# Weight products ordered by part: the high tile's products first, a third high tile, one late weight pool, and held-back gathered rows

## The chip, the core and the metric

The kernel runs on one core of a Trainium2 chip. The metric is the device time of one execution in microseconds (us); less is better. The core has a matrix engine (PE), a vector engine (DVE), a scalar engine (ACT), a general engine (POOL) and an engine that only issues transfers (SP). Each engine takes its instructions in the order in which the program lists them; they wait for each other through semaphores. Transfers are issued from queues (here of SP, ACT and POOL) and share 16 DMA engines. Tiles live in an on-chip memory; matrix results land in eight accumulator banks.

## What is computed

One layer of a hybrid block on 512 tokens of width 2048, in f32, in three parts with a residual and a layer norm after each:

```python
h = hybrid_mixer(x, ...)            # x @ w_in (12 pieces), an mLSTM of 4 heads, forgetting attention of 16 heads,
                                    # two gated branches, and @ w_out
x = layer_norm(DN_ALPHA * x + h, ln_w[l, 0], ln_b[l, 0])
h = memory_cross_attention(x, mem, w_xq, w_xkv, w_xo)   # 4 heads over 256 memory rows
x = layer_norm(DN_ALPHA * x + h, ln_w[l, 1], ln_b[l, 1])
h = peer_ffn(x, w_pq, sub_keys, expert_u, expert_v)     # 16384 experts; each token and head takes its best 16
x = layer_norm(DN_ALPHA * x + h, ln_w[l, 2], ln_b[l, 2])
```

In `peer_ffn` a query picks expert rows by two top-16 searches; the result is `sum_k gelu(u_k . x) * g_k * v_k` over the 128 picked experts of a token.

## The kernel before

**Products in three parts.** PE multiplies a rounded f32 type. To keep f32 accuracy every operand is split into a high part (rounded) and a low part (the rest), and each product is done as high·high + high·low + low·high, three matmuls into one bank (`mm3`, lines 150 to 153). Activations are split once; weights are split as they stream through.

**The weight stream.** All weights come as tiles of 128x1024 f32, 512 KB each. `load_w` (line 136) does this for each tile: SP issues the load into a `raw` tile (line 130); ACT writes the high part `whi` (line 123); DVE (line 126), or POOL (line 125) for every fourth tile while `work["share"]` is 4, subtracts to give the low part `wlo`. Each of `raw`, `whi` and `wlo` is a ring of a few tiles. A slot of `raw` is free for the next load when the subtraction has read it; a slot of `whi` or `wlo` is free when the last matmul that reads it has ended. The ring sizes are set by `weights(stack, raw, hi, lo)`: 5, 2, 2 for the first part (`W_FIRST`), 6, 2, 3 for the second (`W_NEXT`), 3, 2, 2 for the third (line 961) and 5, 2, 2 for the rest (line 996).

**Products of one tile.** `group_as` (line 169) holds an activation block still and streams 512 weight columns: for one block of 128 tokens a tile gives 6 matmuls of 512 columns. `group_ws` (line 155) holds the weights still and streams the tokens: 24 matmuls of 256 or 384 columns. In both, the three products of one pair stand together, so the low tile is wanted right after the first product and the high tile until almost the last.

**Stages.** Path A is the first block of 128 tokens, path B the other 384.

1. Path A through the whole mixer, with the keys and values of the memory made in between (48 groups of 8 weight tiles, most with one token block).
2. The rest of path A (`tail_a`: output product, norms, cross attention, query and top-16 search) interleaved with the mLSTM heads of path B.
3. Path B: branch, attention, merge, output product. Beside it runs the expert sum of path A in `gathered` (line 761): 128 rows of `peer_u` and then 128 of `peer_v` for each of 128 tokens are fetched by POOL with indirect transfers of 1 MB (`rows`, ring of 3), and DVE works each off (lines 770 and 783). `load_w` starts such a row with `rate` rows per weight tile; each is told to wait for the split of the last weight tile. Rows left over are drained by the loop at line 997.
4. First norm, cross attention, output product and second norm of path B (`residual`, `norm`, `cross`). `norm` turns each block on PE and makes the pairs `X2` that the query multiplies. Then the pool `x3`, with the activations and the weight rings, is closed and new rings are opened in the space (line 996).
5. Query and top-16 search of path B, 64 chunks of `stage_a` (line 1089: a chunk of 128 experts times 288 tokens, 2 weight tiles, 48 matmuls into one bank) and the building of the gate table.
6. The dense part: `stage_o` (line 1127) sums 128 chunks of `peer_v` in 256 tiles, with the other 64 chunks of `stage_a` in between. Its raw tiles come from the same ring as those of `stage_a`; its high and low tiles are six slots under one tag. The last 96 tokens of path B are done by gathered rows, beside stages 5 and 6.

A scheduler in the language orders the instructions of each engine by program order and its own estimate of when each can run, so the order of the built program is not the source's in every place.

Of the kernel before, what the change touches and what calls it, by code (L numbers as in the profile page):

```python
# [10 lines left out]
F32 = mybir.dt.float32  # L11
# [10 lines left out]
P = 128  # L22
# [5 lines left out]
ML_H, ML_DK, ML_DV = 4, 256, 512  # L28
FX_H, FX_D = 16, 128
X_H, X_D = 4, 512  # L30
W_FIRST = (5, 2, 2)
W_NEXT = (6, 2, 3)
PH, PKEYS, TOPK = 8, 128, 16
NDENSE = 288
GATHERED = ((64, 64), (32, 32))
# [13 lines left out]
def build(tc, I, out):  # L49
    nc = tc.nc  # L50
    with ExitStack() as ctx:
# [2 lines left out]
        ps = ctx.enter_context(tc.tile_pool(name="ps", bufs=1, space=PSUM))  # L54
        W = {}

        def weights(stack, raw, hi, lo):

            W.update(pool=stack.enter_context(tc.tile_pool(name=f"w{raw}{lo}", bufs=1, reuse_waits="tile")),
                     raw=raw, hi=hi, lo=lo)  # L60

        xs, x0 = ctx.enter_context(ExitStack()), ctx.enter_context(ExitStack())
        xbp = xs.enter_context(tc.tile_pool(name="x_b", bufs=1))
        weights(x0, *W_FIRST)
        xap = x0.enter_context(tc.tile_pool(name="x_a", bufs=1))

        cnt, turn = [0], [0]
# [1 line left out]
        def nm(s):  # L69
            cnt[0] += 1  # L70
            return f"{s}_{cnt[0]}"
# [53 lines left out]
                return nc.gpsimd.tensor_sub(lo, src, hi.bitcast(F32))  # L125
            return nc.vector.tensor_sub(lo, src, hi.bitcast(F32))  # L126

        def load_raw(src, n=1024):
            raw = W["pool"].tile([P, n], F32, tag="raw", bufs=W["raw"], name=nm("raw"))
            nc.sync.dma_start(raw, src)  # L130
            return raw


        work = {"jobs": None, "rate": 0.0, "due": 0.0, "n": 0, "share": 0, "last": None}

        def load_w(src):
            raw = load_raw(src)
            hi = W["pool"].tile([P, 1024], F32R, tag="whi", bufs=W["hi"], name=nm("whi"))
            lo = W["pool"].tile([P, 1024], F32R, tag="wlo", bufs=W["lo"], name=nm("wlo"))
            work["n"] += 1  # L140
            work["last"] = split(hi, lo, raw, work["share"] and work["n"] % work["share"] == 0)
            if work["jobs"] is not None:
                work["due"] += work["rate"]
                while work["due"] >= 1 and work["jobs"] is not None:
                    work["due"] -= 1
                    if next(work["jobs"], None) is None:
                        work["jobs"] = None
            return hi, lo

        def mm3(o, wh, wl, xh, xl, first, last):  # L150
            nc.tensor.matmul(o, wh, xh, start=first, stop=False)  # L151
            nc.tensor.matmul(o, wh, xl, start=False, stop=False)  # L152
            nc.tensor.matmul(o, wl, xh, start=False, stop=last)  # L153

        def group_ws(src, X, n, evac):

            banks = [mm_bank() for _ in range(4)]
            for kt in range(8):
                wh, wl = load_w(src[kt])
                for kk in range(2):  # L160
                    k = 2 * kt + kk
                    xh, xl = X[k]
                    for s in range(4):
                        c = slice(kk * 512 + s * P, kk * 512 + (s + 1) * P)
                        mm3(banks[s][:, :n], wh[:, c], wl[:, c], xh, xl, k == 0, k == 15)
            for s in range(4):
                evac(s, banks[s])

        def group_as(src, X, nt, evac):

            banks = [mm_bank() for _ in range(nt)]
            for kt in range(8):
                wh, wl = load_w(src[kt])
                for t in range(nt):
                    tt = slice(t * P, (t + 1) * P)
                    for kk in range(2):
                        k = 2 * kt + kk
                        xh, xl = X[k]
                        c = slice(kk * 512, (kk + 1) * 512)
                        mm3(banks[t], xh[:, tt], xl[:, tt], wh[:, c], wl[:, c], k == 0, k == 15)  # L180
            for t in range(nt):
                evac(t, banks[t])

# [665 lines left out]
        with tc.tile_pool(name="sa", bufs=1, side="right", reuse_waits="tile") as sa:  # L849
# [162 lines left out]

        with tc.tile_pool(name="topk", bufs=1, reuse_waits="tile") as tp:
            keysT = tp.tile([P, 16, P], F32, tag="keysT", name="keysT")
            nc.gpsimd.dma_start(keysT, I["keysT"])
# [72 lines left out]

        def stage_a(c):

            bank = a_bank()
            for kt in range(2):
                uh, ul = load_w(I["uT"][c, kt])
                for kk in range(8):
                    k = kt * 8 + kk
                    sl = slice(kk * P, (kk + 1) * P)
                    xh, xl = X2[k]
                    mm3(bank[:, :NDENSE], uh[:, sl], ul[:, sl], xh[:, :NDENSE], xl[:, :NDENSE], k == 0, k == 15)
            ga = gap.tile([P, NDENSE], F32, tag="ga", bufs=GA_N, name=nm("ga"))
            nc.scalar.activation(ga, bank[:, :NDENSE], AF.Gelu)  # L1100
            if c in spilled:
                nc.scalar.dma_start(gad[c], ga)
            else:
                gas[c] = ga

        def stage_h(c):
# [20 lines left out]
        def stage_o(c0, q, fill):  # L1127
# [1 line left out]
            banks = [o_bank() for s in range(4)]  # L1129
            last = c0 + J == NC_  # L1130
            for m in range(J // 2):
                raw = load_raw(I["vq"][c0 // 2 + m, q])
                vh, vl = pair(gap, "v", [P, 1024], 6)
                split(vh, vl, raw)
                for j in range(2):
                    c = c0 + 2 * m + j
                    if q == 0:
# [2 lines left out]
                    a, b = hs[c]  # L1140
                    for s in range(4):
                        sl = slice(j * 512 + s * P, j * 512 + (s + 1) * P)
                        mm3(banks[s][:, :NDENSE], vh[:, sl], vl[:, sl], a, b, c == c0, c == c0 + J - 1)
                fill(q * (J // 2) + m)
            if last and q == 0:
                lwd.extend(fin_load(gat))
# [121 lines left out]
```

## Time and profile before

| | us |
|---|---|
| median of 3 runs | 5569.84 (5566.75 to 5576.74) |
| profiled execution, its own time | 5583.58 |
| its span in the trace | 5581.8 |
| PE busy in it | 4928.2 |
| DVE busy | 3723.6 |
| ACT busy | 2111.5 |
| POOL busy | 1686.2 |

Busy time of PE is modelled from pipelined matmuls that overlap, so a busy PE may still lose time at each restart. In a row of the timeline the first number is the start, the second the length, and a bracket gives the engine's idle time before the instruction and what ended it. In a row of the waits the numbers are the sum in us, how often, and the longest. "SPq" is the transfer queue of SP; "x8" counts merged instructions.

### The profile page before, as it was taken

What the parts mean: (1) busy time and instruction counts of PE and PEld (TensorE: products, weight loads), DVE (VectorE), ACT (ScalarE), POOL (GpSimd) and SP (SyncE); (2) the same over time, 40 slices, a digit from 0 to 9 for tenths busy, and PEclk for the clock granted to TensorE, in tenths of its full rate; (3) what the DMA queues carried; (4) which work ended last, traced back from release to release, by engine and by line L of the source; (5) the groups of instructions that cost most, each with busy time, mean ns of one, the idle gap of its engine ahead of it and who ended that gap; (6) DMA issues with size and microseconds to landing.
All of it is one profiled execution on the core that took longest, in us unless ns stands there. A gap on an engine that the chain in (4) does not pass through costs nothing. (4 is left out here: it accounts for less than half of the span.)

```text
span 5581.8 us, 74192 instructions
## 1 busy us (share of the span) xinstructions
PE 4928.2 (88%) x28273; PEld 4418.8 (79%) x28273; DVE 3723.6 (67%) x5275; ACT 2111.5 (38%) x3017; POOL 1686.2 (30%) x1280
## 2 busy tenths in 40 slices
PE   7877777899997899899899797698889999999997
PEld 4656555777776898788797786598888999999996
DVE  7544545454458666665687757579666788887887
ACT  6544554444444222233332322233433433333332
POOL 2222334232224443333355634432001112112222
PEclk9999999999999899999999898799999999999998
DMA  7667777554556777687688668545668899998996
GB/s 235 219 231 227 229 225 237 172 188 164 185 164 213 276 292 287 248 286 252 235 337 326 232 242 308 191 158 189 193 196 309 327 341 361 345 343 337 361 344 242
DMA packets 405190, 1429.35 MB, mean 256 GB/s; under 512 B 93468, under 2 KB 125852, under 8 KB 345664
## 3 DMA queue, kind: packets, MB, share of 16 engines
q1 hardware_dynamic: 242848, 819.80, 42.9%
q0 software_dynamic: 94160, 566.79, 27.3%
q10 hardware_dynamic: 67824, 38.02, 2.4%
q8 instruction: 221, 3.62, 0.3%
q14 instruction: 137, 1.12, 0.1%
HBM read 1351.71 MB, written 72.62 MB: 255 GB/s over the span
## 5 line engine op out<-in xcount | busy, mean ns | idle before, releaser
L123 ACT CAST whi<-raw 128x1024 fp32r<-128x1024 f32 x1216 | 1268.6, 1049 | 1941.1 <-PE mm L153 786.2
L126 DVE TENSOR_TENSOR wlo<-raw,whi 128x1024 fp32r<-128x1024 f32 x976 | 1283.7, 1319 | 963.8 <-ACT whi L123 920.5
L125 POOL TENSOR_TENSOR wlo<-raw,whi 128x1024 fp32r<-128x1024 f32 x240 | 594.6, 2477 | 1159.8 <-ACT whi L123 953.2
L770 DVE SCALAR_TENSOR_TENSOR rows<-rows,xacc 128x2048 f32<-128x2048 f32 x224 | 532.6, 2380 | 277.7 <-DMA rows<-in_peer_u,eid 277.6
L756 POOL DMA_INDIRECT rows<-in_peer_u,eid x224 | 317.1, 1416 | 1141.7 <-DVE wlo L126 403.3
L153 PE MATMUL pa<-Ch,wlo 128*128 128x288 f32 x2048 | 619.2, 303 | 40.6 <-DVE wlo L126 40.0
L151 PE MATMUL pa<-Ch,whi 128*128 128x288 f32 x2048 | 618.3, 302 | 40.9 <-ACT whi L123 32.9
L783 DVE SCALAR_TENSOR_TENSOR xacc<-rows,dots,xacc 128x2048 f32<-128x2048 f32 x224 | 554.4, 2475 | 144.1 <-DMA rows<-in_peer_v,eid 143.2
L152 PE MATMUL pa<-Cl,whi 128*128 128x288 f32 x2048 | 614.6, 300 | 0.0
L151 PE MATMUL po<-hph,vh 128*128 128x288 f32 x2048 | 590.6, 297 | 9.5 <-ACT hph L123 6.8
L152 PE MATMUL po<-hpl,vh 128*128 128x288 f32 x2048 | 595.8, 295 | 0.0
L756 POOL DMA_INDIRECT rows<-in_peer_v,eid x224 | 329.9, 1473 | 843.9 <-DVE xacc L783 338.4
L153 PE MATMUL po<-hph,vl 128*128 128x288 f32 x2048 | 574.4, 295 | 2.7 <-DVE vl L126 2.7
L152 PE MATMUL mm<-wlo,xh 128*128 128x512 f32 x1088 | 457.1, 420 | 123.1 <-POOL wlo L125 65.7
L151 PE MATMUL mm<-xh,whi 128*128 128x384 f32 x1280 | 443.7, 347 | 6.2 <-ACT whi L123 6.2
L151 PE MATMUL mm<-whi,xh 128*128 128x512 f32 x1088 | 420.5, 413 | 31.5 <-ACT whi L123 29.0
L152 PE MATMUL mm<-xl,whi 128*128 128x384 f32 x1280 | 439.0, 343 | 0.0
L153 PE MATMUL mm<-whi,xl 128*128 128x512 f32 x1088 | 437.4, 402 | 0.0
L153 PEld LDWEIGHTS pa<-Ch,wlo 128*128 128x128 f32 x2048 | 394.5, 193 | 50.5 <-DVE wlo L126 49.5
L151 PEld LDWEIGHTS pa<-Ch,whi 128*128 128x128 f32 x2048 | 395.2, 193 | 45.8 <-ACT whi L123 35.1
L153 PE MATMUL mm<-xh,wlo 128*128 128x384 f32 x1280 | 383.2, 347 | 40.4 <-DVE wlo L126 36.6
L152 PEld LDWEIGHTS pa<-Cl,whi 128*128 128x128 f32 x2048 | 395.3, 193 | 0.0
(438 smaller groups left out, 9815.4 us busy)
## 6 DMA issues: line engine op xcount, KB each, us to landing
raw<-in_w_in SPq DMA_DIRECT2D x512, 512.0 KB
raw<-in_uT SPq DMA_DIRECT2D x256, 512.0 KB
raw<-in_vq SPq DMA_DIRECT2D x256, 512.0 KB
raw<-in_w_xkv SPq DMA_DIRECT2D x64, 512.0 KB
raw<-in_w_br_ml SPq DMA_DIRECT2D x64, 512.0 KB
raw<-in_w_br_fx SPq DMA_DIRECT2D x64, 512.0 KB
raw<-in_w_out SPq DMA_DIRECT2D x64, 512.0 KB
raw<-in_w_xq SPq DMA_DIRECT2D x64, 512.0 KB
```

What stands on the lines that cost most here:

```text
L123: nc.scalar.copy(hi, src)
L125: return nc.gpsimd.tensor_sub(lo, src, hi.bitcast(F32))
L126: return nc.vector.tensor_sub(lo, src, hi.bitcast(F32))
L151: nc.tensor.matmul(o, wh, xh, start=first, stop=False)
L152: nc.tensor.matmul(o, wh, xl, start=False, stop=False)
L153: nc.tensor.matmul(o, wl, xh, start=False, stop=last)
L756: i = nc.gpsimd.indirect_dma_start(out=rows, out_offset=None, in_=I[table], in_offset=bass.IndirectOffsetOnAxis(ap=ei[:, k:k + 1], axis=0))
L770: nc.vector.scalar_tensor_tensor(rows, rows, 1.0, xacc, op0=ALU.mult, op1=ALU.mult, accum_out=dots[:, k:k + 1])
L783: nc.vector.scalar_tensor_tensor(xacc, rows, dots[:, k:k + 1], xacc, op0=ALU.mult, op1=ALU.add)
```

## The change

- A new function `products` takes the list of a tile's products and issues all that read the high weight tile, and then all that read the low one. `group_ws`, `group_as`, `stage_a` and `stage_o` use it instead of `mm3`; `mm3` stays for the gates.
- The rings (raw, high, low) are 4, 3, 2 in the first part, 5, 3, 3 in the second, and 3, 2, 2 from the third on to the end, in one pool that is opened ahead of the activations and is not closed. The raw tiles of `stage_o` get a ring of their own with 2 raw, 3 high and 3 low tiles.
- Rows are started at 258/315 per weight tile instead of 258/340, and none during the last two of the four groups of `residual` and until the pairs of `norm` are made (`work["hold"]`).
- The transfer of `keysT` is issued from ACT's queue instead of POOL's.

```diff
-W_FIRST = (5, 2, 2)
-W_NEXT = (6, 2, 3)
...
-        weights(x0, *W_FIRST)
+        weights(x0, "w1", 4, 3, 2)
...
+        def load_pair(src, pool=False, ring=None):
+
+            ring = ring or W
+            raw = load_raw(src, ring=ring)
+            hi = ring["pool"].tile([P, 1024], F32R, tag="whi", bufs=ring["hi"], name=nm("whi"))
+            lo = ring["pool"].tile([P, 1024], F32R, tag="wlo", bufs=ring["lo"], name=nm("wlo"))
+            return hi, lo, split(hi, lo, raw, pool)
...
-            if work["jobs"] is not None:
+            if work["jobs"] is not None and not work["hold"]:
                 work["due"] += work["rate"]
...
+        def products(work, first, last):
+
+            for part in range(2):
+                for i, (o, wh, wl, xh, xl, k, stat) in enumerate(work):
+                    for w, x in ((wl, xh),) if part else ((wh, xh), (wh, xl)):
+                        nc.tensor.matmul(o, w if stat else x, x if stat else w,
+                                         start=k == first and x is xh and not part, stop=k == last and part == 1)
...
-                        mm3(banks[t], xh[:, tt], xl[:, tt], wh[:, c], wl[:, c], k == 0, k == 15)
+                        todo.append((banks[t], wh[:, c], wl[:, c], xh[:, tt], xl[:, tt], 2 * kt + kk, False))
+                products(todo, 0, 15)
...
+                work["hold"] = g >= 2
                 group_as(W[g], X, R.nb, ev)
...
                 split(*o[-1], f)
+            work["hold"] = False
...
-            weights(w2, *W_NEXT)
+            weights(w2, "w2", 5, 3, 3)
...
-        work.update(jobs=gathered(0, 0, P, 0, lambda: work["last"]), rate=258 / 340)
+        work.update(jobs=gathered(0, 0, P, 0, lambda: work["last"]), rate=258 / 315)
...
+        weights(ctx, "w3", 3, 2, 2)
         apool = x3.enter_context(tc.tile_pool(name="acts_a", bufs=1, reuse_waits="tile"))
-        weights(x3, 3, 2, 2)
...
         x3.close()
-        weights(ctx, 5, 2, 2)
...
-            nc.gpsimd.dma_start(keysT, I["keysT"])
+            nc.scalar.dma_start(keysT, I["keysT"])
...
+        V = dict(pool=gap, raw=2, hi=3, lo=3)
...
-                raw = load_raw(I["vq"][c0 // 2 + m, q])
-                vh, vl = pair(gap, "v", [P, 1024], 6)
-                split(vh, vl, raw)
+                vh, vl, _ = load_pair(I["vq"][c0 // 2 + m, q], ring=V)
```

More of the change, by code (lines that the diff above doesn't have):

```diff
@@ L55, in build, with weights @@
         W = {}
-        def weights(stack, raw, hi, lo):
-            W.update(pool=stack.enter_context(tc.tile_pool(name=f"w{raw}{lo}", bufs=1, reuse_waits="tile")),
-                     raw=raw, hi=hi, lo=lo)
+        def weights(stack, name, raw, hi, lo):
+            W.update(pool=stack.enter_context(tc.tile_pool(name=name, bufs=1, reuse_waits="tile")), raw=raw, hi=hi, lo=lo)
         xs, x0 = ctx.enter_context(ExitStack()), ctx.enter_context(ExitStack())
         xbp = xs.enter_context(tc.tile_pool(name="x_b", bufs=1))
-        weights(x0, *W_FIRST)
+        weights(x0, "w1", 4, 3, 2)
         xap = x0.enter_context(tc.tile_pool(name="x_a", bufs=1))
@@ L126, in split, with load_raw @@
             return nc.vector.tensor_sub(lo, src, hi.bitcast(F32))
-        def load_raw(src, n=1024):
-            raw = W["pool"].tile([P, n], F32, tag="raw", bufs=W["raw"], name=nm("raw"))
+        def load_raw(src, n=1024, ring=None):
+            ring = ring or W
+            raw = ring["pool"].tile([P, n], F32, tag="raw", bufs=ring["raw"], name=nm("raw"))
             nc.sync.dma_start(raw, src)
             return raw
-        work = {"jobs": None, "rate": 0.0, "due": 0.0, "n": 0, "share": 0, "last": None}
+        work = {"jobs": None, "rate": 0.0, "due": 0.0, "n": 0, "share": 0, "last": None, "hold": False}
+        def load_pair(src, pool=False, ring=None):
+            ring = ring or W
+            raw = load_raw(src, ring=ring)
+            hi = ring["pool"].tile([P, 1024], F32R, tag="whi", bufs=ring["hi"], name=nm("whi"))
+            lo = ring["pool"].tile([P, 1024], F32R, tag="wlo", bufs=ring["lo"], name=nm("wlo"))
+            return hi, lo, split(hi, lo, raw, pool)
         def load_w(src):
-            raw = load_raw(src)
-            hi = W["pool"].tile([P, 1024], F32R, tag="whi", bufs=W["hi"], name=nm("whi"))
-            lo = W["pool"].tile([P, 1024], F32R, tag="wlo", bufs=W["lo"], name=nm("wlo"))
             work["n"] += 1
-            work["last"] = split(hi, lo, raw, work["share"] and work["n"] % work["share"] == 0)
-            if work["jobs"] is not None:
+            hi, lo, work["last"] = load_pair(src, work["share"] and work["n"] % work["share"] == 0)
+            if work["jobs"] is not None and not work["hold"]:
                 work["due"] += work["rate"]
@@ L159, in group_ws @@
                 wh, wl = load_w(src[kt])
+                todo = []
                 for kk in range(2):
[L161 to L162 removed]
                     for s in range(4):
                         c = slice(kk * 512 + s * P, kk * 512 + (s + 1) * P)
[L165 removed]
+                        todo.append((banks[s][:, :n], wh[:, c], wl[:, c], *X[2 * kt + kk], 2 * kt + kk, True))
+                products(todo, 0, 15)
             for s in range(4):
@@ L173, in group_as @@
                 wh, wl = load_w(src[kt])
+                todo = []
                 for t in range(nt):
@@ L176, in group_as @@
                     for kk in range(2):
-                        k = 2 * kt + kk
-                        xh, xl = X[k]
+                        xh, xl = X[2 * kt + kk]
                         c = slice(kk * 512, (kk + 1) * 512)
-                        mm3(banks[t], xh[:, tt], xl[:, tt], wh[:, c], wl[:, c], k == 0, k == 15)
+                        todo.append((banks[t], wh[:, c], wl[:, c], xh[:, tt], xl[:, tt], 2 * kt + kk, False))
+                products(todo, 0, 15)
             for t in range(nt):
@@ L1142, in stage_o @@
                         sl = slice(j * 512 + s * P, j * 512 + (s + 1) * P)
-                        mm3(banks[s][:, :NDENSE], vh[:, sl], vl[:, sl], a, b, c == c0, c == c0 + J - 1)
+                        todo.append((banks[s][:, :NDENSE], vh[:, sl], vl[:, sl], a, b, c, True))
+                products(todo, c0, c0 + J - 1)
                 fill(q * (J // 2) + m)
```

12 lines of the change are left out of this document (7 added, 5 removed).

## The prediction

> **What bounds the kernel now.** I read the page's slices first, then the stages as windows, then the waits inside each stage, and last the timeline of a few weight tiles.
>
> ```profile
> span 5581.8 us, 74192 instructions
> ...
> PE   7877777899997899899899797698889999999997
> ...
> L783 DVE SCALAR_TENSOR_TENSOR xacc<-rows,dots,xacc 128x2048 f32<-128x2048 f32 x224 | 554.4, 2475 | 144.1 <-DMA rows<-in_peer_v,eid 143.2
> ```
>
> The slices say where PE is short of work: the first quarter, and around slices 24 to 30. The windows put numbers to the stages (length; busy time of PE, PEld, DVE, ACT, POOL with instruction counts; granted clock, DMA share, GB/s):
>
> ```profile
> 0.00:975.00 975.00, 761.41 (x3374) 563.79 (x3374) 527.36 (x741) 502.01 (x665) 304.93 (x250) 0.96 0.71 229
> 975.00:1741.00 766.00, 698.73 (x3149) 562.19 (x3149) 406.83 (x707) 336.64 (x456) 204.90 (x155) 0.98 0.54 177
> 1741.00:3065.00 1324.00, 1208.25 (x6269) 1111.35 (x6268) 881.21 (x1050) 389.68 (x533) 553.97 (x419) 0.96 0.77 278
> 3065.00:3540.00 475.00, 358.41 (x1685) 307.12 (x1683) 335.79 (x301) 131.17 (x197) 240.83 (x184) 0.86 0.72 256
> 3540.00:4264.00 724.00, 639.50 (x4384) 626.82 (x4385) 501.31 (x1269) 262.15 (x552) 110.23 (x84) 0.94 0.60 192
> 4264.00:5500.00 1236.00, 1214.53 (x9089) 1205.24 (x9088) 1008.37 (x1112) 471.18 (x594) 252.82 (x182) 1.00 0.92 347
> ```
>
> ```profile
> 4288.23 0.53 PE po L153 x4
> ```
>
> The last window is the dense part, and PE is its bound: the chain of work that ended last has four matmuls of 288 columns in 0.53 us, 0.133 each, and 9089 times that is 1,209 of 1,236 us. Nothing done for the weights can give more than 27 us there. In the first window no engine is full and DMA is at 0.71, so a chain of waits sets the pace. What ends PE's and ACT's waits in it:
>
> ```profile
> DVE wlo L126 <- ACT whi L123: 338.3, 180, 5.0
> ACT whi L123 <- PE mm L153: 271.5, 230, 4.8
> ...
> PE mm L152 <- POOL wlo L125: 89.4, 62, 3.0
> PE mm L152 <- DVE wlo L126: 62.8, 94, 3.4
> PE mm L151 <- ACT whi L123: 36.5, 42, 2.1
> ```
>
> ACT waits for PE to give a high tile back, PE waits for the parts: a ring that is too short, not an engine that is too slow. Its length is read from the timeline of path A:
>
> ```profile
> 556.98 0.39 PE L151 MATMUL mm<-whi,xh 128*128 128x512 f32 x1
> 557.21 0.39 PE L152 MATMUL mm<-wlo,xh 128*128 128x512 f32 x1
> ```
>
> ```profile
> 557.86 1.05 ACT L123 CAST whi<-raw 128x1024 fp32r<-128x1024 f32 x1 [1.37 <-PE mm L153]
> ```
>
> ```profile
> 559.00 2.35 POOL L125 TENSOR_TENSOR wlo<-raw,whi 128x1024 fp32r<-128x1024 f32 x1 [5.96 <-ACT whi L123]
> ...
> 577.57 2.36 POOL L125 TENSOR_TENSOR wlo<-raw,whi 128x1024 fp32r<-128x1024 f32 x1 [6.04 <-ACT whi L123]
> ```
>
> ```profile
> 556.52 1.23 DVE L126 TENSOR_TENSOR wlo<-raw,whi 128x1024 fp32r<-128x1024 f32 x1 [0.15 <-ACT whi L123]
> ...
> 560.33 2.10 DVE L126 TENSOR_TENSOR wlo<-raw,whi 128x1024 fp32r<-128x1024 f32 x1 [2.58 <-ACT whi L123]
> ```
>
> POOL takes every fourth tile, and one of its subtractions (at 568.67) lies between the two shown: eight tiles in 18.57 us, 2.32 us a tile, 9.29 for four. The same slot of two high tiles sees POOL's subtraction 2.35, six products 1.38 (0.23 apart), a cast 1.05, DVE's subtraction 1.23, six products 1.38 and a cast 1.05: 8.44 us for four tiles, and six handovers of 0.14 make up the 9.29.
>
> **The change, part by part.** Work is neither added nor removed: the same matmuls, casts, subtractions and 512 KB loads. What changes is how late a tile may be.
>
> *First part (rings 4, 3, 2; high products first).* With a third high tile that cycle is gone. The next candidates, for four tiles: PE 4 x 1.38 = 5.5 us; the two low tiles, whose slot is held for a subtraction and two products, 2.35 + 0.46 + 1.23 + 0.46 + 4 x 0.14 = 5.1; and the raw ring of four, where POOL's tile always falls into the same slot. That needs the time of a load:
>
> ```profile
> 13.29 0.33 SPq L130 DMA_DIRECT2D raw<-in_xT  x1
> ```
>
> ```profile
> 16.27 1.33 ACT L123 CAST xh<-raw 128x128 fp32r<-128x128 f32 x4 [0.18 <-DMA raw<-in_xT]
> ```
>
> ```profile
> 16.00:24.00 8.00, 8.00 (x68) 6.79 (x67) 6.51 (x14) 5.34 (x13) 0.00 (x0) 1.00 1.00 371
> ```
>
> From issue to the cast that waited for it: 2.98 us. At the 371 GB/s of a full stretch a tile takes 1.41 us, so with one more load ahead of it 4.39. A raw slot then turns in 2.98 to 4.39 + 1.05 + 2.35 + two handovers, 6.66 to 8.07 us for four tiles, 1.67 to 2.02 a tile. I take the middle, 1.85, since the traffic leaves DMA partly loaded: 0.47 us on each of the 40 x 8 = 320 tiles with one token block is 150 us; the ends are 96 and 208. The memory's 64 tiles carry twice the products of a path A tile and more, and I count nothing for them.
>
> *Second part (5, 3, 3).* Sixteen groups of path A, 128 tiles, are mixed with path B's. The same 0.47 us gives 60; the stage's own rows say 64.6:
>
> ```profile
> PE mm L152 <- DVE wlo L126: 32.4, 35, 3.0
> ...
> PE mm L151 <- ACT whi L123: 18.6, 18, 3.2
> ...
> PE mm L152 <- POOL wlo L125: 13.6, 15, 2.1
> ```
>
> I take 60; by the ends above 38 to 83.
>
> *Path B up to the first norm.* A tile is 18 products of 0.23 us, 4.14. Low first wanted after two thirds of it comes 2.7 us later than now. The waits for low parts:
>
> ```profile
> PE mm L153 <- DVE wlo L126: 38.8, 19, 4.3
> ...
> PE mm L152 <- DVE wlo L126: 13.9, 10, 3.0
> ```
>
> Their means, 2.0 and 1.4 us, are under 2.7; I take 45 of the 52.7, ends 0 and 53. The higher row rate adds 0.060 rows a tile x 2.475 us = 0.15 us of DVE to a tile; DVE is busy 881 of 1,324 us, so that hides in its idle third. Without that cover it would cost 36 us over the 240 tiles here that still start rows.
>
> *Second norm and query (late pool, hold, keysT).*
>
> ```profile
> 3546.97 0.69 PE L151 MATMUL mm<-Ch,whi 128*128 128x384 f32 x1 [49.73 <-ACT whi L123]
> ```
>
> ```profile
> 3530.69 9.48 SPq L832 DMA_DIRECT2D out<-xacc  x2
> 3540.27 2.34 SPq L130 DMA_DIRECT2D raw<-in_peer_wq  x3
> ```
>
> ```profile
> 3544.37 0.54 POOL L1015 DMA_DIRECT2D keysT<-in_keysT  x1
> ```
>
> PE stands 49.73 us before the query, because the first query weights are issued at 3540.27, behind the store of path A's output and into memory of the closed pool. In the built order of the changed kernel 13 query loads stand ahead of that store, and the products of the first query group among the norm's turns. One group of 8 tiles x 24 products x 0.177 us (0.133 scaled from 288 to 384 columns) is 34 us that goes under the norm. Its results still need memory of the closed activations, so the second group starts about when the first does now: late next are the norm's tail on POOL and the gathered rows. The hold does not empty this norm: the drain is built among it and is now longer by 315 against 340, some six rows, 6 us. Gain 28; ends 0 and 45. keysT on ACT stands behind the same memory and blocks ACT where ACT has only the query's results to copy: 0.
>
> *Query to dense part (raw 3 instead of 5).*
>
> ```profile
> PE pa L151 <- ACT whi L123: 32.9, 10, 6.3
> PE pa L153 <- DVE wlo L126: 30.9, 23, 4.8
> ```
>
> A tile is 24 x 0.133 = 3.2 us. High tiles come back a third of a tile earlier, low ones are wanted two thirds later: half of the 63.8, 32. Three raw tiles are 9.6 us against 2.98 + 1.05 + 1.23 for a turn. Ends: 60 gained; 30 lost if six loads take 12 us.
>
> *Dense part (two raw tiles for peer_v).*
>
> ```profile
> ACT vh L123 <- PE po L152: 203.4, 112, 9.1
> ...
> ACT vh L123 <- DMA raw<-in_vq: 51.0, 21, 5.6
> ```
>
> ```profile
> 5101.80 11.98 DMA raw<-in_uT
> ```
>
> 256 tiles in 1,236 us are 4.83 us each. Two raw tiles turn in (2.98 + 1.05 + 1.23 + 0.28)/2 = 2.8 us, or 7.3 with a load as slow as the one shown. Now the cast mostly waits for PE, and for a landing 21 times in 256; three high tiles hold 9.6 us of products. I take 10 lost; ends 15 gained and 51 lost, all landing waits reaching PE.
>
> **Sum.** 150 + 60 + 45 + 28 + 32 - 10 = 305 us. The profiled execution took 5583.58 us, so 5279 for one like it. It stands 13.7 above the median of the runs, 5569.84, so for the median 5265. With all ends: 5106 to 5517.
>
> **A rule against it.** DVE's subtraction at 560.33 took 2.10 us instead of 1.23 and ended 1.08 us after POOL's, which ran until 561.35. The Trainium skill, SBUF — State Buffer, section SBUF: two separate sides, says that the ports which DVE and GpSimd share are locked for a whole instruction, also by a DVE instruction with two SBUF inputs, and the other one blocks; the trace agrees. By it, subtractions that now come closer together exclude each other: 2.35 + 3 x 1.23 = 6.0 us for four tiles, still under the 7.4 that I take, so the forecast stays, and the third rival below gets a floor.
>
> **The rivals.**
> 1. *Loads of peer_v starve the dense part: slower.* At 11.98 us a load the ring turns in 7.3 us, 2.4 over 4.83; x 256 is 625 lost, less the 315 won elsewhere: 5880. It decides from 1.23 us a tile, a sustained load time of 9.6 us. DMA at 0.92 speaks for it; only 21 casts waiting now, for it against. 7%.
> 2. *The low parts stay late because DVE works in order:* softmax, searches and rows ahead of a subtraction delay it as now. Then only the lower ends in the first two parts are won, 134, less 10: 5446. The waits for wlo <- whi on DVE speak against it, as its delay was mostly ACT's. 20%.
> ```profile
> L125 POOL TENSOR_TENSOR wlo<-raw,whi x95: 2340/2362/2924, 28.1 to 973.3; 128x1024 fp32r<-128x1024 f32 x95
> ```
>
> 3. *The raw ring never binds:* path A runs at the subtractions' 1.5 us: 262 in the first part, 105 in the second, and the upper ends elsewhere, 158: 5045. By the lock, DVE's 527 and POOL's subtractions (95 x 2.36 = 224) can't overlap, so the first part is at least 751 us and 224 is its most: then 5083. 10%.
> 4. *The order is undone by the scheduler:* in the built order path A's tiles have four products with whi and then two with wlo, so not there. It is so for the hold in the second norm, which is priced at nothing.
>
> **How the numbers follow.** Forecast 60%, the rivals 20, 10 and 7%, and 3% that the parts cancel within 0.2%, about what a measurement of this kernel can tell from no change. Faster 0.90, same 0.03, slower 0.07. The range leaves out the first rival and most of the third: 5100 to 5450.
>
> **What would show it.** The first part's window ends near 825 instead of 975, POOL's subtractions of path A 7.4 us apart, and "ACT whi <- PE" under 100 us there. PE's gap before the query is gone, with query products between the norm's turns. The dense part keeps some 1,240 us and "PE po <- vh" stays under 20 us. Wrong would be: low tiles ending PE's waits as often as now, or PE in the dense part waiting for vh behind landings.

## The result and the profile after

The changed kernel takes 5386.67 us against 5573.29 us for the kernel before on the same chip (medians): ratio 0.9676, 95% interval 0.964 to 0.9713. On the median that the prediction starts from, 5569.84, that is 5389 us; 5265 was forecast, with a range of 5100 to 5450. The execution that was profiled took 5381.62 us, with a span of 5379.9.

First the page's slices of the changed kernel (40 equal slices, PE's busy tenths) and the windows by stage (length; busy time of PE, PEld, DVE, ACT, POOL with instruction counts; granted clock, DMA share, GB/s):

```profile
span 5379.9 us, 74574 instructions
...
PE   7988889999988999998997986999899999998886
```

```profile
0.00:865.00 865.00, 736.40 (x3403) 551.55 (x3404) 530.83 (x745) 508.35 (x671) 307.34 (x250) 0.97 0.76 258
865.00:1552.00 687.00, 665.39 (x3129) 551.20 (x3128) 411.31 (x635) 327.31 (x452) 214.18 (x152) 1.00 0.57 198
1552.00:2817.00 1265.00, 1176.70 (x6254) 1093.70 (x6255) 921.71 (x1124) 385.37 (x531) 575.90 (x425) 0.96 0.80 296
2817.00:3398.00 581.00, 475.95 (x2420) 428.50 (x2419) 404.37 (x486) 174.53 (x250) 249.75 (x200) 0.91 0.65 237
3398.00:3968.00 570.00, 517.20 (x3793) 509.17 (x3792) 446.45 (x1081) 228.32 (x506) 82.10 (x63) 0.96 0.65 213
3968.00:5280.00 1312.00, 1225.37 (x8882) 1201.11 (x8880) 991.96 (x1095) 462.19 (x581) 241.18 (x177) 0.98 0.84 319
```

The front is fuller and the end is emptier: the last four slices, 9, 9, 9 and 7 before, show 8, 8, 8 and 6. To compare kernels whose stages end at other times I cut every trace at the same five events: the first `w_out` load, the last `peer_wq` load of path A, path B's first `w_xq` load, the first `stage_a` matmul and the first `stage_o` matmul of the dense part. The same cuts carry the forecast's six terms:

| stage | before, us | after, us | change | forecast |
|---|---|---|---|---|
| first part | 976 | 865 | -111 | -150 |
| second part | 764 | 684 | -80 | -60 |
| path B to its first norm | 1325 | 1268 | -57 | -45 |
| norms, cross part and query | 629 | 604 | -25 | -28 |
| query to dense part | 579 | 544 | -35 | -32 |
| dense part to the end | 1309 | 1415 | +106 | +10 |
| span | 5582 | 5380 | -202 | -305 |

Five stages became shorter by 308 us together, 315 forecast; the sixth gave a third of it back. What ends the waits in the first part now:

```profile
ACT whi L120 <- DMA raw<-in_w_in: 147.2, 150, 3.7
...
ACT whi L120 <- PE mm L163: 73.5, 51, 2.7
...
PE mm L163 <- ACT whi L120: 42.8, 62, 2.4
PE mm L163 <- POOL wlo L122: 37.8, 37, 6.2
...
PE mm L163 <- DVE wlo L123: 23.1, 34, 2.7
```

ACT waits for landings (147.2 us) where it waited for PE (271.5): the raw ring of four is the short one now. In the dense part:

```profile
ACT whi L120 <- DMA raw<-in_vq: 387.1, 143, 10.7
...
PE po L163 <- ACT whi L120: 39.0, 28, 9.2
...
PE po L163 <- DVE wlo L123: 33.2, 31, 3.5
```

The cast of a `peer_v` tile waits for its landing 143 times where it was 21 times, and PE waits behind it. Two stretches of the dense part as windows show where, first one with both kinds of tile, then one after the last `uT` tile:

```profile
3968.00:4860.00 892.00, 882.54 (x6614) 876.74 (x6613) 674.35 (x719) 339.40 (x433) 154.89 (x110) 1.00 0.86 328
```

```profile
4960.00:5280.00 320.00, 262.15 (x1704) 246.58 (x1704) 248.20 (x284) 90.03 (x109) 61.50 (x47) 0.93 0.81 304
```

6614 matmuls in 892 us are 7.41 a us; 1704 in 320 are 5.33. At 24 matmuls a tile, 30.9 tiles and 22.2 tiles in 100 us. In the kernel before the last `stage_a` matmul stood 109 us before the end of the span (5473 of 5582), now it stands 467 before it (4913 of 5380): the `uT` tiles have run ahead, and 93 of the 256 `peer_v` tiles, 18 before, are left to run alone at the slower pace. From 4913 to the last product of `stage_o` at 5344 that loses 431 x (1 - 5.33 / 7.41) = 121 us, about what the stage has lost.

### The profile page after: what moved, and what is told of

Read it like the earlier page. It is cut to its first block, busy times and chain, and to the rows that moved or that the text cites. A ratio compares the mean times of both kernels' runs of the same rounds, so it can differ in the third digit from the quotient of the medians.

```text
span 5379.9 us, 74574 instructions
## 1 busy us (share of the span) xinstructions
PE 4856.5 (90%) x28273; PEld 4387.9 (82%) x28273; DVE 3778.6 (70%) x5275; ACT 2109.8 (39%) x3016; POOL 1691.1 (31%) x1279
## 3 DMA queue, kind: packets, MB, share of 16 engines
q1 hardware_dynamic: 242848, 819.80, 42.8%
## 5 line engine op out<-in xcount | busy, mean ns | idle before, releaser
L120 ACT CAST whi<-raw 128x1024 fp32r<-128x1024 f32 x1472 | 1536.2, 1051 | 2373.0 <-PE mm L163 990.2
L123 DVE TENSOR_TENSOR wlo<-raw,whi 128x1024 fp32r<-128x1024 f32 x1232 | 1603.5, 1311 | 893.5 <-ACT whi L120 516.0
L163 PE MATMUL po<-hph,whi 128*128 128x288 f32 x2048 | 570.1, 304 | 55.6 <-ACT whi L120 39.9
L163 PE MATMUL pa<-Ch,whi 128*128 128x288 f32 x2048 | 567.2, 301 | 41.0 <-ACT whi L120 39.6
L163 PE MATMUL po<-hpl,whi 128*128 128x288 f32 x2048 | 563.2, 301 | 0.0
L163 PEld LDWEIGHTS po<-hph,whi 128*128 128x128 f32 x2048 | 394.1, 194 | 69.7 <-ACT whi L120 49.1
L163 PEld LDWEIGHTS po<-hpl,whi 128*128 128x128 f32 x2048 | 395.0, 194 | 0.0
L163 PE MATMUL mm<-wlo,xh 128*128 128x512 f32 x1088 | 327.4, 410 | 47.7 <-POOL wlo L122 26.1
L163 PE MATMUL po<-hph,wlo 128*128 128x288 f32 x2048 | 336.5, 300 | 34.8 <-DVE wlo L123 34.7
L163 PE MATMUL pa<-Ch,wlo 128*128 128x288 f32 x2048 | 327.4, 297 | 6.3 <-DVE wlo L123 6.3
```

What stands on the lines that cost most here:

```text
L120: nc.scalar.copy(hi, src)
L163: nc.tensor.matmul(o, w if stat else x, x if stat else w, start=k == first and x is xh and not part, stop=k == last and part == 1)
```

## The experiments

Each ratio is to the kernel before on the same chip (5573 to 5592 us). The stages, in us, by the same cuts:

| kernel | 1st | 2nd | B | query | to dense | dense | ratio |
|---|---|---|---|---|---|---|---|
| before | 976 | 764 | 1325 | 629 | 579 | 1309 | 1 |
| after | 865 | 684 | 1268 | 604 | 544 | 1415 | 0.9676 |
| e1 old product order | 885 | 694 | 1283 | 617 | 504 | 1509 | 0.9801 |
| e2 old rings, first two parts | 797 | 714 | 1296 | 608 | 544 | 1431 | 0.9611 |
| e3 old late pool and `peer_v` ring | 876 | 686 | 1268 | 634 | 555 | 1299 | 0.9503 |
| e4 four raw tiles for `peer_v` | 877 | 682 | 1269 | 611 | 534 | 1335 | 0.9475 |
| b1 new product order alone | 791 | 714 | 1325 | 633 | 554 | 1300 | 0.9484 |
| b2 two high tiles again | 874 | 713 | 1283 | 609 | 541 | 1430 | 0.9743 |
| b3 late pool undone | 871 | 681 | 1273 | 635 | 552 | 1424 | 0.9714 |
| b4 recombined | 790 | 691 | 1271 | 596 | 533 | 1337 | 0.9354 |
| c1 b4, row rate 258 / 340 | 790 | 689 | 1280 | 618 | 535 | 1336 | 0.9428 |
| c2 b4, hold off | 791 | 690 | 1276 | 553 | 533 | 1334 | 0.9258 |
| c3 b4, three raw for `peer_v` | 787 | 690 | 1274 | 601 | 533 | 1354 | 0.9371 |
| d1 c2, row rate 258 / 290 | 788 | 689 | 1273 | 553 | 533 | 1340 | 0.9260 |

Stages that an edit doesn't touch differ by up to some 12 us; differences of that size are not read.

The cut ahead of the dense part moves with the order in which PE takes its tiles. Ahead of the first `stage_o` product, PE has done 62.5 chunks of `stage_a` in the kernel before, 63.5 in the changed one, 62 to 65 in the others, but only 51 in e1, and a chunk is 48 x 0.133 = 6.4 us. So, where it matters, the last two stages are also cut at equal work: at the 3072nd product of `stage_a` and `stage_o` together, which is 64 chunks' worth.

| kernel | first `stage_a` product to the 3072nd product | from there to the end |
|---|---|---|
| before | 589 | 1299 |
| after | 547 | 1412 |
| e1 | 587 | 1426 |
| e3 | 550 | 1304 |
| e4 | 548 | 1321 |
| b1 | 549 | 1305 |

**e1, the products in the old order, all else changed.**

```diff
-            for part in range(2):
-                for i, (o, wh, wl, xh, xl, k, stat) in enumerate(work):
...
+            for o, wh, wl, xh, xl, k, stat in work:
+                if stat:
+                    mm3(o, wh, wl, xh, xl, k == first, k == last)
+                else:
+                    mm3(o, xh, xl, wh, wl, k == first, k == last)
```

> The changed kernel with the three products of a pair side by side again; rings, pools and rows stay changed. Theory (the third high tile carries the gain of the first part, the order of products the gain of path B, and the two raw tiles for peer_v the loss in the dense part): first part 865 to about 890 us, path B up to its cross attention about 40 longer, the dense part still some 100 us over before; about 5460 us in all. Rival (the new order itself costs the dense part its 106 us): the dense part falls back by about 100 us, and the whole stays at or under 5400.

5489.42 us, 0.9801 [0.9777, 0.9825]. The order is worth some 1.3% here. By the first table, of the 112 us of span beside the changed kernel, 94 lie in the dense part, with 40 gained in the stage ahead of it. That is the cut, since 12.5 chunks moved from the one to the other: at equal work the old order costs 40 us ahead of the dense part (587, 547) and 14 in it (1426, 1412). The rest is 20 in the first part, 10 in the second, 15 in path B, where the theory had 40, and 12 in the stage with the query. The rival, that the new order makes the loss of the dense part, is refuted. With rings of 4, 3, 2 the first part is nearly as short with the old order (885) as with the new (865 to 877).

**e2, the rings of before in the first two parts, all else changed.**

```diff
-        weights(x0, "w1", 4, 3, 2)
+        weights(x0, "w1", 5, 2, 2)
...
-            weights(w2, "w2", 5, 3, 3)
+            weights(w2, "w2", 6, 2, 3)
```

> The changed kernel with rings 5, 2, 2 and 6, 2, 3 in the first two parts, as before; everything else stays changed. Theory: the cycle through two high tiles comes back, but high tiles are now free after four of six products, 0.46 us earlier, so path A's four tiles take about 9.29 - 0.9 = 8.4 us: the first part is 870 to 910 us, the second 20 to 40 us longer, about 5430 in all. Rival (the third high tile alone carried it): first part back at 975, about 5530 in all.

5383.48 us, 0.9611 [0.9586, 0.9635]: theory and rival both had it slower than the changed kernel, and it is not (0.9676 there). The first part is 68 us shorter than with three high tiles (797 against 865), the second 30 longer. The waits of ACT in its first part, 0 to 797 us:

```profile
ACT whi L120 <- PE mm L163: 128.1, 139, 3.0
...
ACT whi L120 <- DMA raw<-in_w_in: 28.7, 40, 2.3
```

With five raw tiles the wait for landings is 28.7 us instead of 147.2, and the high ring of two costs ACT 128 us of waiting that hardly reaches PE, which waits 14.4 us for high tiles there and 42.8 in the changed kernel. So order and third high tile do the same work in the first part, and the tile is paid for with a raw tile that is worth more. The theory failed because it kept both subtractions in the cycle; with the high products first, PE can issue four of a tile's six products before its low tile is there. That reading fits 797, but no run separates it from the earlier release of the high tile.

**e3, the late pool and `peer_v`'s own ring undone** (3, 2, 2 in the activations' stack, then 5, 2, 2 shared by `uT` and `peer_v` raw tiles), **and e4, four raw tiles for `peer_v` from the main pool**, both with all else changed. The edit of e3, then that of e4:

```diff
-        weights(ctx, "w3", 3, 2, 2)
         apool = x3.enter_context(tc.tile_pool(name="acts_a", bufs=1, reuse_waits="tile"))
+        weights(x3, "w3", 3, 2, 2)
...
         x3.close()
+        weights(ctx, "w4", 5, 2, 2)
...
-                vh, vl, _ = load_pair(I["vq"][c0 // 2 + m, q], ring=V)
+                raw = load_raw(I["vq"][c0 // 2 + m, q])
+                vh = gap.tile([P, 1024], F32R, tag="whi", bufs=3, name=nm("vh"))
+                vl = gap.tile([P, 1024], F32R, tag="wlo", bufs=3, name=nm("vl"))
+                split(vh, vl, raw)
```

```diff
-            raw = ring["pool"].tile([P, n], F32, tag="raw", bufs=ring["raw"], name=nm("raw"))
+            raw = ring.get("rawpool", ring["pool"]).tile([P, n], F32, tag="vraw" if "rawpool" in ring else "raw", bufs=ring["raw"], name=nm("raw"))
...
-        V = dict(pool=gap, raw=2, hi=3, lo=3)
+        V = dict(pool=gap, rawpool=mn, raw=4, hi=3, lo=3)
```

> The changed kernel with the late pool and peer_v's own rings undone: rings 3, 2, 2 closed with the activations, then 5, 2, 2, with one raw ring for both tables. Theory: the dense part loses its 106 us, and the query waits again for its first weights, some 25 us: about 5310 us in all, with uT loads spread to the end. Rival (product order makes the loss): dense part as long as in the changed kernel, about 5410.

> The changed kernel with four raw tiles for peer_v instead of two, in the pool that is opened when the dense part begins; nothing else. Theory: a tile of peer_v then turns in half the time, the stage_a tiles run less far ahead, and the dense part is 70 to 100 us shorter: 5290 to 5320 us. Rival (product order): unchanged, 5387.

5319.52 us, 0.9503 [0.9483, 0.9522], and 5303.66 us, 0.9475 [0.9456, 0.9494], both as the theory had it. The dense part is 1299 with the shared ring and 1335 with four tiles. The `uT` tiles still run ahead in e4 (last `stage_a` matmul 256 us before the end of the span, 117 in e3), but ACT hardly waits for landings while `peer_v` runs alone. The same wait, first in e4 from 5070 to 5270 us, then in the changed kernel from 4960 to 5280:

```profile
ACT whi L120 <- DMA raw<-in_vq: 22.8, 12, 7.1
```

```profile
ACT whi L120 <- DMA raw<-in_vq: 178.8, 59, 10.7
```

So the short ring costs some 80 us of the dense part, 91 at equal work (1412, 1321). The run-ahead that comes with a ring of its own costs 17 us more at equal work (1321, 1304), little over what stages vary by; the 36 of the first table (1335, 1299) are in part the cut.

**b1, the kernel before with the new product order alone.** All other edits undone.

> The kernel before with one edit: every tile's products with the high part first (all rings, the late pool, the held rows, the row rate and the key load as before). Theory now held (with a high tile free after four of six products, two high tiles are enough; five raw tiles then set the pace): first part 797 instead of 976 as with the old rings in the changed kernel, second part 715 instead of 764, path B some 35 shorter, dense part about 1300: 5592 - 179 - 49 - 35 = about 5330 us, 0.953 (5300 to 5360). Rival (the third high tile or the later edits are needed beside the order): first part over 860 and more than 5420 us.

5298.4 us, 0.9484 [0.9466, 0.9502]: faster than the whole change, and just under its theory's 5300 to 5360. First part 791, second 714, as with the old rings in e2. In path B it won nothing, 1325 against 1325. PE's waits there, 1506 to 2834 us:

```profile
PE mm L163 <- DVE wlo L123: 42.3, 30, 5.2
PE mm L163 <- ACT Hh L120: 30.0, 4, 23.2
```

The waits for a low tile are nearly as many as before, 30 for 42.3 us where it was 29 for 52.7 (38.8 + 13.9): that the product is wanted 2.7 us later helped little, and no run shows why.

**b2, two high tiles again in the changed kernel** (4, 2, 2 and 5, 2, 3).

```diff
-        weights(x0, "w1", 4, 3, 2)
+        weights(x0, "w1", 4, 2, 2)
...
-            weights(w2, "w2", 5, 3, 3)
+            weights(w2, "w2", 5, 2, 3)
```

> The changed kernel with two high tiles in place of three in the first two parts, everything else of it kept (rings 4, 2, 2 and 5, 2, 3). Theory (in the first part the raw ring of four sets the pace, by its turn of load, cast and subtraction; the third high tile gives nothing there): first part 865 to 890, total within 25 us of the changed kernel, 5375 to 5430. Rival (the third high tile is worth a raw tile: it only looks worthless because it was paid for with one): first part 930 to 975, total about 5470.

5443.66 us, 0.9743 [0.972, 0.9766]. The first part is 874 us, in the theory's 865 to 890: there the third high tile gives nothing, the raw ring of four sets the pace. The total is above the theory's 5375 to 5430, because the tile does work in the second part (713 without it, 684 with it) and a little in path B (1283, 1268). From six raw tiles to five nothing changes in the second part (714 in b1, 713 here).

**b3, the late pool undone in the changed kernel**, `peer_v`'s ring of two kept (3, 2, 2 in the activations' stack, then 3, 2, 2).

> The changed kernel with the late weight pool undone (3, 2, 2 in the activations' stack, closed before the dense part's pool of 3, 2, 2), peer_v's own ring of two raw tiles kept. Theory (the two raw tiles of peer_v cost the dense part its 106 us; the late pool lets the first query group go under the norm): about 50 us gap ahead of the query back, stage from the last path B weights to the first dense matmul 25 longer, dense part still 1400 to 1430: 5405 to 5430 us. Rival (the place of the pool makes the weights of the uT tiles run ahead): dense part 1300 to 1340 and 5300 to 5340 us.

5431.03 us, 0.9714 [0.9691, 0.9737], by the theory, a little over its range. The dense part stays at 1424, so the pool's place does not make the `uT` tiles run ahead; the stage with the query is 31 us longer (635, 604).

**b4, recombined:** 5, 2, 2 in the first part, four raw tiles for `peer_v`, the rest as changed.

> Recombination: high part first, five raw and two high tiles in the first part (5, 2, 2), 5, 3, 3 in the second, late pool, hold and row rate as changed, four raw tiles for peer_v. Theory (the parts add): first part 797 instead of 877, the rest as in the run with four raw tiles for peer_v: 5304 - 80 = 5225 us, 0.934 (5205 to 5260). Rival (the gain of the first part is given back in the second, as with the old rings, where the second was 30 longer): 5250 to 5290 us.

5222.44 us, 0.9354 [0.9338, 0.9369]. The parts add.

**c1, c2 and c3, each one edit on b4.**

```diff
-        work.update(jobs=gathered(0, 0, P, 0, lambda: work["last"]), rate=258 / 315)
+        work.update(jobs=gathered(0, 0, P, 0, lambda: work["last"]), rate=258 / 340)
```

```diff
-                work["hold"] = g >= 2
+                work["hold"] = False
```

```diff
-        V = dict(pool=gap, rawpool=mn, raw=4, hi=3, lo=3)
+        V = dict(pool=gap, rawpool=mn, raw=3, hi=3, lo=3)
```

> The recombined kernel (5, 2, 2 then 5, 3, 3, four raw tiles for peer_v) with the row rate back at 258 / 340, the hold kept. With the product order alone path B's stage (its first weights to its first w_xq load) stayed at 1326 us against 1325 before; in every kernel with the new rate and hold it is 1268 to 1296. Theory (the rate does it, by putting the rows elsewhere among the subtractions): stage 1271 back to 1295 to 1310, total 5245 to 5265, 0.940. Rival (the third high tile does it alone): stage 1265 to 1280, total 5215 to 5235.

> The recombined kernel with the hold off, the new row rate kept. Theory (priced at nothing, since rows that are not held back do not end PE's waits there; the drain after the norm gets shorter): 5210 to 5235 us, 0.933 to 0.938. Rival (the hold keeps DVE free for the last subtractions and the norm): norm stages 20 to 30 longer, 5240 to 5260 us.

> The recombined kernel with three raw tiles for peer_v instead of four. Theory (two tiles fail because a turn of load, cast and subtraction, some 7 to 8 us, takes more than the 6.4 us of products of two tiles; three have 9.6): dense part within 20 us of the 1337 with four, total 5220 to 5245. Rival (the loss falls evenly with the ring, as the uT tiles run ahead by so much less): dense part about 1375, total about 5260.

c1: 5265.28 us, 0.9428 [0.9409, 0.9446]. The total is at the upper end of the theory, but its place is not: path B's stage is 1280, as the rival had it, and not 1295 to 1310; the larger loss is in the stage with the query, 618 against 596.

c2: 5176.18 us, 0.9258 [0.9242, 0.9274]: neither the theory nor the rival, 46 us better than b4, and 43 of them in the stage with the query (553 against 596). The rows explain it. Of the 128 that are started from path B on, the updates of `xacc` that DVE had made when the query's weights were first issued were 90 in c1, 107 in b4 and 128 in c2. What is held back is drained after the norm, and its end stands on ACT ahead of the copies that free the query's banks. First PE's wait, then ACT's, in b4 (columns: total us, times, longest):

```profile
PE mm L163 <- ACT qT L737: 32.2, 1, 32.2
```

```profile
ACT fst L200 <- DVE fst L199: 42.3, 1, 42.3
```

`fst` at L200 belongs to the layer norm of the drained rows: ACT waits 42.3 us for the last row's statistics, the `qT` copies stand behind it in ACT's order, and PE has no bank for the second query group. In c2 PE waits for `qT` at no place, and the longest waits of that stretch are

```profile
PE sm L608 <- DVE ra L604: 19.5, 2, 13.0
PE mm L163 <- DVE wlo L123: 14.8, 10, 3.7
```

c3: 5238.16 us, 0.9371 [0.9355, 0.9386], as the theory said: three raw tiles keep most of it (dense part 1354 against 1337 with four and 1415 with two), though the `uT` tiles run further ahead than with four (last `stage_a` matmul 340 us before the end of the span, 256 in b4). The loss does not fall evenly with the ring, which fits a loss that is there when a turn of the ring is longer than the products of its tiles.

**d1, c2 with a row rate of 258 / 290.**

> The recombined kernel with the hold off and a still higher row rate, 258 / 290. Theory (what the rows cost is the number of them left when the query's weights begin: 38 of 128 at rate 340 with hold, 21 at 315 with hold, none at 315 without): none are left already, so nothing is won: within 12 us of the kernel with the hold off, 5165 to 5190. Rival (every row moved forward is worth time, since DVE has idle time in path B): 5140 to 5160 us.

5176.88 us, 0.926 [0.9242, 0.9278], as the theory said: with no row left over, nothing is won by starting rows sooner. c2 and d1 are the best versions; against the whole change (0.9676) they keep its product order, third high tile in the second part and late pool, and c2 its row rate.

## Why the prediction was right and where it was wrong

The sign held and the time is in the range; the forecast was 124 us too low, 5265 against 5389. By its steps:

- **First part, 150 forecast, 111 measured.** That the raw ring of four would be the next bound is shown (b2, and the landings that end ACT's waits). Its load time was undersized: 2.98 to 4.39 us was taken, 4.6 is the median from issue to landing. The profile page's DMA issues (the last number is that median):

```profile
raw<-in_w_in SPq DMA_DIRECT2D x512, 512.0 KB, 4.6
raw<-in_vq SPq DMA_DIRECT2D x256, 512.0 KB, 5.6
```

  By the prediction's formula 4.6 + 1.05 + 2.35 + 0.28 = 8.28 for four, 2.07 a tile, and 0.25 x 320 = 80 us; 111 were won. The rest comes from where the prediction started: its 2.32 us was read in a fast stretch. From one cast of ACT to the next, a tile of path A took 2.55 us on the mean of the first part before and 2.17 after, near the 2.07 of the formula; over 320 tiles that is 122 us, where the cut at the first `w_out` load shows 111. A tile of the memory took 2.33 and 2.38, so nothing was won there, as counted. Four of POOL's subtractions, each every fourth tile, are 8.1 us apart on the mean in the stretch below (479.80 to 504.19), and 8.4 in the median of the first part, not 7.4:

```profile
479.80 2.38 POOL L122 TENSOR_TENSOR wlo<-raw,whi 128x1024 fp32r<-128x1024 f32 x1 [5.88 <-ACT whi L120]
...
504.19 2.37 POOL L122 TENSOR_TENSOR wlo<-raw,whi 128x1024 fp32r<-128x1024 f32 x1 [1.67 <-ACT whi L120]
```

  "With a third high tile that cycle is gone" holds (e1: 885), but the step left out that the new order alone removes the cycle too, and does so better (791), because it leaves five raw tiles. The new rings cost 74 us here.
- **Second part, 60 forecast, 80 measured.** 50 of it are the order's (b1), 30 the third high tile's (b2 to after). Right in mechanism, undersized.
- **Path B, 45 forecast, 57 measured, for the wrong reason.** The forecast gave it to the order, which alone won nothing here (b1); that the sum came close is luck. In the changed kernel PE's wait for DVE's low tiles is nearly gone in this stage:

```profile
PE mm L163 <- ACT Hh L120: 35.3, 4, 27.4
...
PE mm L163 <- DVE wlo L123: 4.3, 4, 1.8
```

  The third high tile gives some 15 of the 57 (1283 to 1268), the row rate 9 at most (c1), and both are hardly more than the stages vary. What makes the rest, between b1's 1325 and e2's 1296 with the same rings, stays open. It is won ahead of the first `w_out` load of path B, which comes 1191 us into the stage in b1 and 1159 in e2. The hold and the key load act only later, so the row rate and the late pool are left, and in other settings each was worth little: 9 us (c1) and 5 (b3).
- **Norms and query, 28 forecast, 25 measured.** The gap of 49.73 us went, as forecast, and the late pool is worth about the 31 us of b3. What was late next was mispriced. The hold was priced at "some six rows, 6 us"; it leaves 21 rows, and it costs 43 us in the recombined kernel (c2). And a wait of 36.8 us took the gap's place, through ACT, so the nearness of 25 to 28 is partly luck. The forecast had seen that ACT could be blocked by memory not yet free and priced it 0, since only the query's copies stand behind; but those copies free the banks that PE needs. It was not the key load that blocked it: in the changed kernel a weight cast waits 36.04 us for the store of the norm's output, the next, whose landing is of `peer_v`, 8.57, and the last step of the drained rows, `fst`, 6.06 more; only then come the copies:

```profile
3291.70 1.04 ACT L120 CAST whi<-raw 128x1024 fp32r<-128x1024 f32 x1 [36.04 <-DMA x2d<-ra]
3301.32 1.04 ACT L120 CAST whi<-raw 128x1024 fp32r<-128x1024 f32 x1 [8.57 <-DMA raw<-in_vq]
...
3308.43 0.20 ACT L200 ACTIVATE fst<-fst 128x1 f32<-128x1 f32 x1 [6.06 <-DVE fst L199]
3308.54 1.60 ACT L737 COPY qT<-mm 128x384 f32<-128x384 f32 x4
```

```profile
3309.05 0.69 PE L163 MATMUL mm<-Ch,whi 128*128 128x384 f32 x1 [36.84 <-ACT qT L737]
```

  The hold was not taken out of the changed kernel by itself. There the two casts stand ahead of the copies as well, so the 43 us of c2 are not shown for it.
- **Query to dense part, 32 forecast, 35 measured.** It is the order's, as forecast: at equal work the stage is 589 us before, 549 with the order alone (b1), 547 in the changed kernel and 587 in it with the old order (e1).
- **Dense part, 10 lost forecast, 106 measured: the step that failed.** "256 tiles in 1,236 us are 4.83 us each" took it that the two kinds of tile alternate to the end, so that a turn of 2.8 us has room. With a ring of its own `peer_v` is no longer held in step with `uT`; in the built order `uT` runs ahead, and then a `peer_v` tile is wanted every 24 x 0.133 = 3.2 us. The turn measures 5.6 + 1.05 + 1.23 + 0.28 = 8.16 us, 4.08 for each of two tiles and 2.72 for each of three: two are too few, and three nearly suffice, as c3 shows. (The 22.2 tiles in 100 us are 4.5 us a tile, so this turn leaves some 0.4 us of each tile unexplained.) The failure has the place and the mechanism of the first rival, at a sixth of its price: 106 us instead of 625, as only the last 93 tiles run alone. It is also what the prediction named as a sign of being wrong: PE waiting for high tiles of `peer_v` behind landings (39.0 us, where under 20 was forecast).
- **The other rivals.** Low parts that stay late behind DVE's other work: not seen in the first part, where DVE's low tiles end 23.1 us of PE's waits and it was 62.8; in path B the order alone left most of these waits (b1). A raw ring that never binds: refuted by the 147.2 us of landings. An order undone by the scheduler: not so for the products, but for the order of `uT` and `peer_v` the built order decided the result.
- **The rule against it.** The Trainium skill (SBUF — State Buffer, section SBUF: two separate sides) says that DVE and GpSimd share a pair of ports, which a GpSimd instruction or a DVE one with two SBUF inputs holds for its whole length while the other blocks. The changed kernel shows it again, in POOL's subtraction of 495.42 to 497.80 us and DVE's before and behind it:

```profile
495.42 2.38 POOL L122 TENSOR_TENSOR wlo<-raw,whi 128x1024 fp32r<-128x1024 f32 x1 [3.66 <-PE sm L496]
```

```profile
494.08 1.23 DVE L123 TENSOR_TENSOR wlo<-raw,whi 128x1024 fp32r<-128x1024 f32 x1 [0.45 <-ACT whi L120]
...
497.21 1.68 DVE L123 TENSOR_TENSOR wlo<-raw,whi 128x1024 fp32r<-128x1024 f32 x1 [1.27 <-ACT whi L120]
```

  Alone 1.23 us; begun 0.59 us before POOL's end it ended 1.09 us after it, 1.68 in all: nearly all its work came after POOL's.

So five terms had the right sign, not all for the reason given. The order alone (0.9484) is worth more than the whole change (0.9676): four raw tiles in the first part (74 us), two for `peer_v` (some 80) and perhaps the hold (43 in the recombined kernel) took more than the other edits gave. The time is in the range because that left 185 us on the slower side: the dense part's error alone is 96 us and the first part's 39, and 32 came back where the second part and path B won more than forecast.

## What to carry to other kernels

Price each slot of a ring by the ring that binds: turn = landing + cast + subtraction, over the number of slots, against the time of one tile's products in the stretch where that stream runs alone, not on the mean of the stage. Before giving memory for another high tile, try whether an earlier last use frees the old ones, since a reorder costs no slot. Work that is held back is not gone: ask on which in-order engine its last step will stand, and what is queued behind it. When stages are compared between kernels, check that the cuts have the same work on each side.

## What was not expected of the hardware

The median time from issue to landing of a 512 KB tile, over all loads of a kind, is no constant: for `w_in` it was 4.6 us in the changed kernel, with four raw tiles in the first part, and 4.8 in b1 with five; for `peer_v` 5.6 with a ring of two, 6.8 with four (b4) and 7.4 with the shared five (b1). The rows for b1, from the profile page's DMA issues:

```profile
raw<-in_w_in SPq DMA_DIRECT2D x512, 512.0 KB, 4.8
raw<-in_uT SPq DMA_DIRECT2D x256, 512.0 KB, 4.9
raw<-in_vq SPq DMA_DIRECT2D x256, 512.0 KB, 7.4
```

With more slots, and so more loads under way at once, each load was longer here, and the ring's gain was less than its number of slots says: from four to five raw tiles the formula with 4.6 us gives 0.41 us a tile, 132 us over 320 tiles, and 74 to 87 were measured (865 to 877 down to 790). With five tiles landings still end 28.7 us of ACT's waits (e2), but the high ring's 128 us stand beside them, so how much of the shortfall is the longer load and how much the next bound was not separated.
